# RWKV-7 and sliding-window decoder step: 16-row triangular inverses with a TensorE merge, and a third bonus buffer

## The chip, the cores and the metric

The kernel runs on one core of a Trainium2 chip. The metric is the device time of one execution in microseconds (us). The change is compared by the medians of runs made alike. The engines are TensorE (PE in the views; PEld is its weight load), VectorE (DVE), ScalarE (ACT), GpSimd (POOL) and SyncE (SP), which here issues almost all DMAs.

## The reference

One layer of a decoder for a prompt of 1024 tokens and eight samples of 8 tokens (1088 columns in all). A normalised input goes through one projection; half of its width feeds an RWKV-7 recurrence with 8 heads of 64, the other half attends within a window of 128. Both results are gated, projected, gated again and normalised. What matters here is the recurrence over tokens:

```python
    def step(S, inp):
        r_t, w_t, k_t, v_t, kk_t, a_t = inp
        sa = jnp.einsum('bhvk,bhk->bhv', S, kk_t)
        S = (S * w_t[:, :, None, :] - sa[..., None] * (kk_t * a_t)[:, :, None, :]
             + v_t[..., None] * k_t[:, :, None, :])
        return S, jnp.einsum('bhvk,bhk->bhv', S, r_t)
    ...
    S_fin, y = lax.scan(step, S0.astype(f32), xs)
    ...
    mixed = jnp.concatenate([o_r * jax.nn.silu(gate_r), o_a * jax.nn.silu(gate_a)], axis=-1)
    h = h + mixed @ w_out
    gate = jax.nn.sigmoid(rmsnorm(h, g_ple) @ w_pg)
    h = h + gate * (p @ w_pp)
```

## The kernel before, in words

**Stages.** The input is loaded, normalised and split into a high and a low part (`xh`, `xl`), so that each large product is three TensorE products (`gemm`, L157): high by high, low by high, high by low. `acc_k`, `acc_v`, `acc_q` and `acc_z` are projections; attention is interleaved with `acc_z`. Then come the recurrence (`chain`) and, around it, work that doesn't need its order: the gates (`acc_ga` and `acc_gr`, 12 groups of 24 products each) and the output part (`Late`: `acc_wa`, `acc_wr`, `acc_wg`, `pp`, and the final normalisation), whose weights pass through DRAM (`wo_dh`, `wo_dl`: half-megabyte stores, loaded back later). The products of the gates and of the output part, 128 x 128 by 384 or 320 columns, 1728 in all, are called gate products here.

**The chain.** The 1024 tokens are 16 chunks of 64. `steps` runs them one after the other: `ch` = state by `L` (L962); VectorE copies that to `rh` (L964); TensorE multiplies `rh` by the inverse in `B` (`ch<-rh`, L967); ScalarE and VectorE put the result into `sv`; TensorE multiplies `sv` by `K` (`cs`, L974), and VectorE adds that to the scaled state `sg`, which gives the next `sv`. "Step 9" is the ninth chunk, and its `ch<-rh` is the instruction by which the text dates it. `y`, the chunk's output, is normalised later (`finish`, from L918), where `bvl` is loaded and added as the bonus term.

**The inverse.** `prepare(u)` makes the operands of unit u: four chunks for u = 0 to 3, and the eight samples as one chunk for u = 4. Products `gram` give masked matrices `L` and `B`; per chunk and head there is a triangular 64 x 64 matrix to invert. In L836 to L896 this is done so: its diagonal 32 x 32 blocks (64 per unit, each twice with every other column of the inverse: 128 partitions) go through DRAM (`at_d`) into `a2` (called `a` in the views). VectorE eliminates row by row: 31 steps of a product into `tm` and a subtraction into `ti`, 62 instructions, recorded under the helper's line L55. ScalarE copies the result (`to`, L867), it goes through DRAM (`tt_d`, L869) back into `B` (L872), and the two blocks are merged: a transpose (L879), TE (L883), a copy `es` (L886), TF (L891) and a copy into `B` (L894). `a2`, `ti` and `tm` have one buffer each; `B`, `L` and `K` lie in two rings, unit u using ring u % 2, so unit 2 can only start when unit 0's steps have been read out of it.

**What sets the order.** `ORDER` = "P0 P1 V0 S0 P2 S1 P3 S2 G4 H0 P4 X4 S3" (L329) is the order in which the program is written: P is `prepare`, S `steps`, G the gates, H the late part, X the sample. The tile framework then schedules: it moves instructions within every engine's queue by its own timeline, with the chain's instructions at high priority. The program on each engine is therefore a fixed list, executed in order; an instruction that waits holds up all behind it on its engine. So where gate products stand between the chain's instructions was settled when the kernel was built.

## Time and profile before

| what | value |
|---|---|
| runs | 935.97, 939.41, 939.56 us |
| median | 939.41 us |
| profiled execution, its own time | 942.16 us |
| its span (first to last instruction) | 940.4 us |
| busy share PE / DVE / ACT / POOL | 88 / 67 / 40 / 39% |

The profile is one execution; its span is what all views divide. A busy share is a mean over stages with different limits, so the stages have to be read apart. In a table by stretch each line is one window: its length, the busy time of each engine with the number of its instructions in brackets, the granted clock of TensorE as a share of 2.4 GHz, the busy share of the DMA engines and GB/s. A timeline row is a start in us, a duration in us, the engine, the line of the kernel, the operation and its tiles; x16 are sixteen records in a row put into one. A product of 32-bit floats leaves two records. In the chain of waits each row is the start, the duration and what held the end.

### The profile page before, as it was taken

What the parts mean: (1) busy time and instruction counts of PE and PEld (TensorE: products, weight loads), DVE (VectorE), ACT (ScalarE), POOL (GpSimd) and SP (SyncE); (2) the same over time, 40 slices, a digit from 0 to 9 for tenths busy, and PEclk for the clock granted to TensorE, in tenths of its full rate; (3) what the DMA queues carried; (4) which work ended last, traced back from release to release, by engine and by line L of the source; (5) the groups of instructions that cost most, each with busy time, mean ns of one, the idle gap of its engine ahead of it and who ended that gap; (6) DMA issues with size and microseconds to landing.
All of it is one profiled execution on the core that took longest, in us unless ns stands there. A gap on an engine that the chain in (4) does not pass through costs nothing.

```text
span 940.4 us, 17475 instructions
## 1 busy us (share of the span) xinstructions
PE 828.5 (88%) x6352; PEld 738.4 (79%) x6352; DVE 632.7 (67%) x1511; ACT 372.5 (40%) x864; POOL 369.3 (39%) x494
## 2 busy tenths in 40 slices
PE   6978999999998989899799965987687989999994
PEld 5878999878886679788688854876577887899983
DVE  7856487777777453468774769588959766854464
ACT  6202086666666442652233332511333443322131
POOL 8548466665676422314231314315433353200000
PEclk9989999999999999899899975899797999999996
DMA  8013201322135447647644499686556879998882
GB/s 292 23 61 101 66 23 57 91 91 77 59 91 156 112 94 167 169 127 171 163 118 123 117 258 316 140 267 182 174 148 223 292 274 329 306 328 278 272 294 82
DMA packets 146007, 157.81 MB, mean 168 GB/s; under 512 B 59288, under 2 KB 115864, under 8 KB 145656
## 3 DMA queue, kind: packets, MB, share of 16 engines
q1 hardware_dynamic: 145104, 155.57, 54.6%
q10 hardware_dynamic: 816, 1.11, 0.4%
q8 instruction: 50, 0.82, 0.4%
q14 instruction: 37, 0.30, 0.1%
HBM read 106.77 MB, written 49.67 MB: 166 GB/s over the span
## 4 chain that ended last, share of the span: by engine, by line
PE 43%; DVE 25%; DMA 14%; ACT 6%; issue 6%; SPq 4%; POOL 2%; DVEq 0%; ACTq 0%; POOLq 0%
PE acc_z L157 6%; PE acc_gr L157 4%; PE acc_q L157 3%; DVE ti L55 3%; PE pp L1348 2%; DVE tm L55 2%; DMA a<-at_d 2%; ACT s L425 2%; PE ov L446 2%; PE acc_wg0g L157 1%; PE acc_wg3g L157 1%; DVE xl L58 1%; PE acc_wg7g L157 1%; PE acc_wg4g L157 1%; DVE s L421 1%
## 5 line engine op out<-in xcount | busy, mean ns | idle before, releaser
L157 PE MATMUL acc_z<-xh,wh_z 128*128 128x384 f32 (+1 forms) x312 | 65.1, 340 | 0.0
L157 PE MATMUL acc_z<-xl,wh_z 128*128 128x384 f32 (+1 forms) x312 | 62.6, 331 | 0.0
L157 PE MATMUL acc_z<-xh,wl_z 128*128 128x384 f32 (+1 forms) x312 | 62.5, 331 | 0.0
L157 PEld LDWEIGHTS acc_z<-xh,wh_z 128*128 128x128 f32 x312 | 53.7, 192 | 1.7 <-ACT pTS L505 0.2
L157 PEld LDWEIGHTS acc_z<-xh,wl_z 128*128 128x128 f32 x312 | 52.3, 188 | 1.0 <-issue 0.2
L157 PEld LDWEIGHTS acc_z<-xl,wh_z 128*128 128x128 f32 x312 | 52.6, 189 | 0.5
L55 DVE TENSOR_TENSOR ti<-ti,tm 128x56 f32<-128x56 f32 (+28 forms) x152 | 50.2, 330 | 3.5
L55 DVE TENSOR_TENSOR tm<-a,ti 128x56 f32<-128x56 f32 (+28 forms) x152 | 50.2, 330 | 3.5
L55 POOL TENSOR_TENSOR sg<-sv,GC 64x256 f32<-64x256 f32 x32 | 20.9, 652 | 63.0 <-DVE sv L55 61.1
L64 POOL TENSOR_SCALAR s<-s,sm 128x256 f32<-128x256 f32 (+1 forms) x64 | 34.6, 557 | 17.2 <-ACT pT L444 4.6
L1187 ACT ACTIVATE q<-hx 128x384 f32<-128x384 f32 (+1 forms) x41 | 20.8, 507 | 51.8 <-DVE hx L55 19.4
L800 PE MATMUL gram<-L,K 64*128 64x128 f32 x272 | 31.4, 324 | 4.9 <-issue 3.3
L55 POOL TENSOR_TENSOR wl_z<-wr_z,wh_z 128x1024 fp32r<-128x1024 f32 x13 | 31.3, 2406 | 10.1 <-ACT wh_z L146 4.8
L800 PEld LDWEIGHTS gram<-L,K 64*128 64x128 f32 x272 | 27.0, 219 | 9.5 <-issue 6.5
L55 DVE TENSOR_TENSOR zr<-acc_z,R 128x384 f32<-128x384 f32 (+2 forms) x52 | 21.7, 434 | 18.5 <-PE acc_z L157 18.2
L55 DVE TENSOR_TENSOR sq<-sq,q 128x384 f32<-128x384 f32 (+1 forms) x41 | 22.6, 552 | 15.1 <-ACT q L1187 14.7
L425 ACT ACTIVATE s<-s,sm 128x256 f32<-128x256 f32 (+1 forms) x64 | 30.9, 485 | 1.9 <-DVE sm L62 1.9
L446 PE MATMUL ov<-pT,vtok 128*64 128x512 f32 x60 | 31.2, 638 | 0.4 <-ACT pT L444 0.4
L1358 ACT ACTIVATE t<-t 128x384 f32<-128x384 f32 (+3 forms) x25 | 12.2, 494 | 46.8 <-DVE t L55 46.8
L55 POOL TENSOR_TENSOR gsa<-gsa,goa 128x384 f32<-128x384 f32 (+1 forms) x12 | 11.8, 985 | 45.8 <-DVE ti L55 27.0
L804 ACT COPY B<-L 64x512 f32<-64x512 f32 x34 | 20.9, 616 | 20.8 <-DVE L L55 19.9
L55 DVE TENSOR_TENSOR L<-gram,cst 128x512 f32<-128x512 f32 x34 | 22.5, 684 | 8.2 <-PE gram L800 8.0
(622 smaller groups left out, 2445.7 us busy)
## 6 DMA issues: line engine op xcount, KB each, us to landing
wr_z<-in_wz SPq DMA_DIRECT2D x13, 512.0 KB
L<-kq_d SPq DMA_DIRECT2D x24, 256.0 KB
sv<-vt_d SPq DMA_DIRECT2D x32, 128.0 KB
wh_wo<-wo_dh SPq DMA_DIRECT2D x8, 512.0 KB
wl_wo<-wo_dl SPq DMA_DIRECT2D x8, 512.0 KB
raw<-in_xT SPq DMA_DIRECT2D x8, 384.0 KB
kq_d<-KQ SPq DMA_DIRECT2D x8, 384.0 KB
bk_d<-BK SPq DMA_DIRECT2D x8, 384.0 KB
```

What stands on the lines that cost most here:

```text
L55: e.tensor_tensor(out, a, b, op=op)
L58: V.scalar_tensor_tensor(out, a, s, b, op0, op1)
L64: e.tensor_scalar(out, a, s1, s2, op0, op1)
L157: PE.matmul(acc[:, :n], w_[:, k0 + k, :], a_[c][:, k, :n], start=i + k == 0, stop=i == 2 and k == K - 1)
L421: V.tensor_tensor_reduce(s[:, j, :nk], sc[:, jj, :nk], mask, 1.0, -3e38, ADD, MAX, mx[:, j:j + 1])
L425: S.activation(s[:, j, :nk], s[:, j, :nk], AF.Exp, bias=m[:, 0, j:j + 1], accum_out=m[:, 2, j:j + 1])
L446: PE.matmul(ov[own, :], vtok[:, blk, own], pT[g].rearrange("p a b -> p (a b)"), start=pos == 0, stop=pos == nb - 1)
L800: PE.matmul(Gp[h][:, p], bk[hs, p], L[h][hs, p], start=True, stop=True)
L804: S.copy(r.B[hs, ci], L[h][hs])
L1187: e.S.square(q, h)
L1348: PE.matmul(pa, w[:, i], p[:, i], start=i + j == 0, stop=i == 1 and j == len(pr) - 1)
L1358: S.activation(t, t, AF.Tanh, scale=0.5)
```

## The change

The elimination works on 16 x 16 blocks: 128 of them fill the 128 partitions, with 16 columns each, and 15 steps take the place of 31. Two 16-row inverses then are merged into one of 32 rows in the way in which two of 32 are merged into one of 64: a product TC (L887 of the changed kernel), copies (`e1`), a product TD (L894), and copies with the factor -1 into `B`. TC and TD are 64 products of 16 x 16 each per unit, spread over four quadrants of TensorE's array. For them, transposed and plain 16 x 16 blocks are fetched from DRAM into `tq` by eight loads (L878, L879); `tt_d` gives way to `t1_d`, and the inverse goes back to `at_d` into its diagonal blocks. `fill` is no longer called in the elimination at steps 19 and 27, as there are none. The sample's 8-row matrices need no merge, and it returns before TC, TE and TF. Beside this, `bvl` has three buffers instead of two.

```diff
--- before.py
+++ after.py
@@ -744,13 +744,13 @@
     MUL, ADD, SUB, MAX = ALU.mult, ALU.add, ALU.subtract, ALU.max
     cst, par, ident, dp = e.cst, e.par, e.ident, e.dp
     kp = e.kp
-    early = ("a2", "ti", "tm", "rn", "q2")
+    early = ("a2", "ti", "tm", "rn", "q2", "tq")
     tl = lambda shape, tag, name, bufs: (kp if tag in early else e.kp3 if tag in ("sv", "sg", "rh") else e.kp2).tile(
         shape, F32, tag=tag, name=name, bufs=bufs)
     LO, HI = slice(0, 64), slice(64, 128)
 
     at_d = [dp.tile([64 if u < 4 else 16, 32, 32], F32, name=f"at_d{u}") for u in range(5)]
-    tt_d = [dp.tile([64 if u < 4 else 16, 32, 32], F32, name=f"tt_d{u}") for u in range(5)]
+    t1_d = [dp.tile([64 if u < 4 else 16, 16, 16], F32, name=f"t1_d{u}") for u in range(5)]
 
     units = [list(range(4 * u, 4 * u + 4)) for u in range(4)] + [[16]]
     src = lambda ch: (ch // 6, ch % 6)
@@ -827,49 +827,73 @@
         ncp = 4 * nch
         Bv = r.B.rearrange("p c a b -> p (c a) b")[:, :ncp]
         at4 = at_d[u].rearrange("(c r b) s t -> r b s c t", r=2, b=2)
-        tt4 = tt_d[u].rearrange("(c r b) s t -> r b s c t", r=2, b=2)
+        t14 = t1_d[u].rearrange("(c r b) t s -> r b t c s", r=2, b=2)
+        diag = lambda d, q: d[..., 16 * q:16 * q + 16, 16 * q:16 * q + 16]
         rows = lambda pr, b: slice(64 * pr + 32 * b, 64 * pr + 32 * b + 32)
-        a2 = tl([128, 32, 32], "a2", f"a2_{u}", 1)
-        rn = tl([128, 32], "rn", f"rn{u}", 1)
-        HO = max(H, 32)
-        P2 = slice(0, 2 * HO)
-        for x in range(0, 2 * HO, H):
-            DMAQ("rn").dma_start(rn[x:x + H], e.ss_d[chs[0]:chs[0] + nch].rearrange("c p r (b t) -> (c p r b) t", b=2))
+        row16 = lambda pr, b: slice(64 * pr + 32 * b, 64 * pr + 32 * b + 16)
+        quad = [(pr, b) for pr in range(2) for b in range(2)]
+        a2 = tl([128, 16, 16], "a2", f"a2_{u}", 1)
+        rn = tl([128, 16], "rn", f"rn{u}", 1)
+        P2 = slice(0, 2 * H)
+        HQ = [slice(H * q, H * q + H) for q in range(2)]
+        for q in range(2):
+            DMAQ("rn").dma_start(rn[HQ[q]], e.ss_d[chs[0]:chs[0] + nch].rearrange(
+                "c p r (b q t) -> q (c p r b) t", b=2, q=2)[q])
         ts(V, rn[P2], rn[P2], 1e-24, None, MAX)
         V.reciprocal(rn[P2], rn[P2])
-        for pr in range(2):
-            for b in range(2):
-                DMAQ("at").dma_start(at4[pr, b], Bv[rows(pr, b), :, 32 * b:32 * b + 32])
-        for x in range(0, 2 * HO, H):
-            DMAQ("at").dma_start(a2[x:x + H], at_d[u])
-        ti = tl([128, 32, 16], "ti", f"ti{u}", 1)
+        for pr, b in quad:
+            DMAQ("at").dma_start(at4[pr, b], Bv[rows(pr, b), :, 32 * b:32 * b + 32])
+        for q in range(2):
+            DMAQ("at").dma_start(a2[HQ[q]], diag(at_d[u], q))
+        ti = tl([128, 16, 16], "ti", f"ti{u}", 1)
         G.memset(ti[P2], 0.0)
 
-        tif = ti.rearrange("p t c -> p (t c)")
-        for h in range(2):
-            hh = slice(HO * h, HO * h + HO)
-            G.tensor_copy(tif[hh, 16 * h:16 * h + 496:33], rn[hh, h::2])
-        tt(V, a2[P2], a2[P2], rn[P2].unsqueeze(1).to_broadcast([2 * HO, 32, 32]), MUL)
-        tm = tl([128, 136], "tm", f"tm{u}", 1)
-        for j in range(31):
-            e_ = (j | 7) + 1 if smp else 32
-            c0 = (j // 8) * 4 if smp else 0
-            nr, ncol = e_ - j - 1, j // 2 + 1 - c0
+        G.tensor_copy(ti.rearrange("p t c -> p (t c)")[P2, 0::17], rn[P2])
+        tt(V, a2[P2], a2[P2], rn[P2].unsqueeze(1).to_broadcast([2 * H, 16, 16]), MUL)
+        tm = tl([128, 64], "tm", f"tm{u}", 1)
+        for j in range(15):
+            e_ = (j | 7) + 1 if smp else 16
+            c0 = (j // 8) * 8 if smp else 0
+            nr, ncol = e_ - j - 1, j + 1 - c0
             if nr == 0:
                 continue
             w = tm[P2, 0:nr * ncol].rearrange("p (a b) -> p a b", a=nr)
-            tt(V, w, a2[P2, j, j + 1:e_].unsqueeze(2).to_broadcast([2 * HO, nr, ncol]),
-               ti[P2, j, c0:c0 + ncol].unsqueeze(1).to_broadcast([2 * HO, nr, ncol]), MUL)
+            tt(V, w, a2[P2, j, j + 1:e_].unsqueeze(2).to_broadcast([2 * H, nr, ncol]),
+               ti[P2, j, c0:c0 + ncol].unsqueeze(1).to_broadcast([2 * H, nr, ncol]), MUL)
             tt(V, ti[P2, j + 1:e_, c0:c0 + ncol], ti[P2, j + 1:e_, c0:c0 + ncol], w, SUB)
             if fill and j % 8 == 3:
                 e.fill(("t", u))
-        to = tl([128, 16, 32], "q2", f"to{u}", 2)
+        to = tl([128, 16, 16], "q2", f"to{u}", 2)
         S.copy(to[P2].rearrange("p c t -> p t c"), ti[P2])
-        for h in range(2):
-            DMAQ("tt").dma_start(tt_d[u].rearrange("i (c h) t -> h i c t", h=2)[h], to[HO * h:HO * h + H])
-        for pr in range(2):
-            for b in range(2):
-                DMAQ("tt").dma_start(Bv[rows(pr, b), :, 32 * b:32 * b + 32], tt4[pr, b])
+        for q in range(2):
+            DMAQ("tt").dma_start(diag(at_d[u], q), to[HQ[q]])
+        for pr, b in quad:
+            DMAQ("tt").dma_start(Bv[rows(pr, b), :, 32 * b:32 * b + 32], at4[pr, b])
+        if smp:
+            return r
+
+        DMAQ("tt").dma_start(t1_d[u], ti[HQ[0]])
+        tq = tl([128, 2, 16, 16], "tq", f"tq{u}", 1)
+        for pr, b in quad:
+            DMAQ("tt").dma_start(tq[row16(pr, b), 0], t14[pr, b])
+            DMAQ("tt").dma_start(tq[row16(pr, b), 1], at4[pr, b, 16:32, :, 16:32])
+        e1 = tl([128, 16, 16], "q2", f"e1_{u}", 2)
+        bank = lambda nm: ps("ov", nm, 1)[:, 0:256].rearrange("p (a b) -> p a b", a=16)
+        up = lambda b: slice(32 * b + 16, 32 * b + 32)
+        p1 = bank(f"TC{u}")
+        for i in range(ncp):
+            for pr, b in quad:
+                a = row16(pr, b)
+                PE.matmul(p1[a, i], Bv[a, i, up(b)], tq[a, 0, i], start=True, stop=True)
+        for pr, b in quad:
+            S.copy(e1[row16(pr, b)], p1[row16(pr, b)])
+        p2 = bank(f"TD{u}")
+        for i in range(ncp):
+            for pr, b in quad:
+                a = row16(pr, b)
+                PE.matmul(p2[a, i], e1[a, i], tq[a, 1, i], start=True, stop=True)
+        for pr, b in quad:
+            S.activation(Bv[row16(pr, b), :, up(b)], p2[row16(pr, b)], AF.Copy, scale=-1.0)
 
         t1 = tl([128, 16, 32], "q2", f"t1_{u}", 2)
         es = tl([128, 16, 32], "q2", f"es_{u}", 2)
@@ -933,7 +957,7 @@
             y = ys[ci]
             tt(G, y, y, w[:, ci].unsqueeze(2).to_broadcast([128, 4, 64]), MUL)
             tt(G, y, y, lnw, MUL)
-            bv = tl([128, 4, 64], "bv", f"bvl{ch}", 2)
+            bv = tl([128, 4, 64], "bv", f"bvl{ch}", 3)
             DMAQ("bvl").dma_start(bv, e.vt_d[ch % 2, ch // 2].rearrange("h t p v -> (h t) p v"))
             tt(V, bv, bv, bq[:, ci].unsqueeze(2).to_broadcast([128, 4, 64]), MUL)
             tt(V, y, y, bv, ADD)
```

**VectorE, end of unit 0's elimination.** `L_3683<-gram_7` and `L_3684<-gram_7` are the masked matrices of the fourth chunk of unit 1. Before:

```order
L55 TENSOR_TENSOR L_3683<-gram_7_4033,cst 128x512
L55 TENSOR_TENSOR tm_3811<-a_0_3794,ti_3806 128x126
L55 TENSOR_TENSOR L_3684<-gram_7_4034,cst 128x512
L55 TENSOR_TENSOR ti_3806<-ti_3806,tm_3811 128x21x6
L55 TENSOR_TENSOR gsa_6183<-acc_ga_2_6158,R 128x320
L55 TENSOR_TENSOR tm_3811<-a_0_3794,ti_3806 128x120
L55 TENSOR_TENSOR ti_3806<-ti_3806,tm_3811 128x20x6
```

There nineteen more pairs follow. After the change the same place reads:

```order
L55 TENSOR_TENSOR tm_3810<-a_0_3794,ti_3806 128x28
L55 TENSOR_TENSOR ti_3806<-ti_3806,tm_3810 128x2x14
L55 TENSOR_TENSOR L_3683<-gram_7_4149,cst 128x512
L55 TENSOR_TENSOR tm_3810<-a_0_3794,ti_3806 128x15
L55 TENSOR_TENSOR L_3684<-gram_7_4150,cst 128x512
L55 TENSOR_TENSOR ti_3806<-ti_3806,tm_3810 128x15
L55 TENSOR_TENSOR gsa_6647<-acc_ga_2_6622,R 128x320
```

The pair on 15 elements beside `L` is the last one of unit 0.

**TensorE behind step 8, after the change.** `TC_5216` and `TD_5285` are unit 2's, `cs_5639` is step 8, and the `ch<-rh` of step 9 stands some thirty rows further on:

```order
L1014 MATMUL cs_5639<-sv_5586,B_3686 64x64 x8
L157 MATMUL acc_gr_0_7113<-xh_78,wh_gr_7078 128x384 x4
L157 MATMUL acc_gr_0_7113<-xl_81,wh_gr_7078 128x384 x8
L157 MATMUL acc_gr_0_7113<-xh_78,wl_gr_7079 128x384 x5
L887 MATMUL TC_5216<-tq_5206,B_3690 16x16 x61
L157 MATMUL acc_gr_0_7113<-xh_78,wl_gr_7079 128x384 x3
L157 MATMUL acc_gr_1_7144<-xh_79,wh_gr_7072 128x384 x8
L157 MATMUL acc_gr_1_7144<-xl_82,wh_gr_7072 128x384 x8
L157 MATMUL acc_gr_1_7144<-xh_79,wl_gr_7073 128x384 x3
L800 MATMUL gram_14_5798<-L_3683,K_3685 128x128
L800 MATMUL gram_14_5799<-L_3684,K_3685 128x128
L894 MATMUL TD_5285<-tq_5206,e_2_5215 16x16 x64
```

So gates of `acc_gr` stand between TC and TD of unit 2, where `acc_wa` of the late part stood before.

**SP, the loads of `tq` for unit 3, after the change.** `wh_woa` and `wl_woa` are late weights on their way to DRAM:

```order
L869 DMA at_d_3676<-to_5895 64x16x16
L1046 DMA L_3688<-kq_d 64x512 x2
L1328 DMA wo_dh<-wh_woa_7853 128x2x512
L1328 DMA wo_dl<-wl_woa_7854 128x2x512
L1328 DMA wo_dh<-wh_woa_7861 128x2x512
L878 DMA tq_5904<-t_d_3681 16x16x16 x3
L871 DMA B_3686<-at_d_3676 32x16x32 x4
L879 DMA tq_5904<-at_d_3676 16x16x16 x3
L878 DMA tq_5904<-t_d_3681 16x16x16
L879 DMA tq_5904<-at_d_3676 16x16x16
```

Three half-megabyte stores are issued between the store of the inverse and the loads that follow it (`t_d` is the program's `t1_d`).

## Rows read from the trace of the kernel before

**Rows 1.** The page, busy time, share of the span and instructions.

```profile
PE 828.5 (88%) x6352; PEld 738.4 (79%) x6352; DVE 632.7 (67%) x1511; ACT 372.5 (40%) x864; POOL 369.3 (39%) x494
```

**Rows 2.** Table by stretch: length, PE, PEld, DVE, ACT, POOL, PEclk, DMA share, GB/s.

```profile
0.00:470.00 470.00, 429.89 (x2669) 380.24 (x2670) 315.73 (x712) 223.72 (x557) 242.99 (x343) 0.97 0.39 110
470.00:554.00 84.00, 79.48 (x1002) 68.56 (x1001) 51.90 (x129) 28.23 (x61) 21.33 (x34) 0.96 0.52 137
554.00:611.00 57.00, 40.08 (x405) 34.90 (x402) 43.22 (x107) 24.45 (x52) 20.43 (x26) 0.73 0.83 239
611.00:731.00 120.00, 93.07 (x1153) 81.87 (x1151) 97.74 (x280) 33.98 (x66) 43.78 (x52) 0.87 0.64 195
731.00:940.00 209.00, 185.99 (x1134) 172.81 (x1132) 124.11 (x286) 62.11 (x128) 40.76 (x40) 0.96 0.81 276
```

**Rows 3.** Timeline of TensorE, the products of steps 8 and 9.

```profile
554.44 0.68 PE L967 MATMUL ch<-rh,B 64*64 64x64 f32 x16
...
611.53 0.68 PE L967 MATMUL ch<-rh,B 64*64 64x64 f32 x16
```

**Rows 4.** Timeline of VectorE, `rh` of steps 6 and 7.

```profile
530.70 0.42 DVE L964 COPY rh<-ch 128x256 f32<-128x256 f32 x1 [2.14 <-PE ch L962]
...
541.13 0.42 DVE L964 COPY rh<-ch 128x256 f32<-128x256 f32 x1 [0.97 <-PE ch L962]
```

**Rows 5.** Table by stretch for tile `ti`: DVE, ACT, POOL, PEclk, DMA, GB/s.

```profile
0.00:940.00 940.00, 100.35 (x304) 5.57 (x5) 5.06 (x15) 0.94 0.55 168
554.00:611.00 57.00, 23.26 (x54) 1.10 (x1) 0.94 (x3) 0.73 0.83 239
611.00:731.00 120.00, 32.46 (x118) 2.28 (x2) 0.94 (x3) 0.87 0.64 195
```

**Rows 6.** Timeline of VectorE, unit 2's elimination.

```profile
566.29 2.68 DVE L55 TENSOR_TENSOR tm<-a,ti 128x133 f32<-128x133 f32 x1
...
574.43 0.29 DVE L55 TENSOR_TENSOR ti<-ti,tm 128x136 f32<-128x136 f32 x1
...
588.01 0.17 DVE L55 TENSOR_TENSOR ti<-ti,tm 128x16 f32<-128x16 f32 x1
```

**Rows 7.** Timeline of VectorE, unit 0's elimination and the transpose behind it.

```profile
408.60 0.18 DVE L55 TENSOR_TENSOR tm<-a,ti 128x31 f32<-128x31 f32 x1
...
412.57 0.25 DVE L55 TENSOR_TENSOR tm<-a,ti 128x81 f32<-128x81 f32 x1
...
420.83 0.68 DVE L55 TENSOR_TENSOR L<-gram,cst 128x512 f32<-128x512 f32 x1
...
440.93 0.17 DVE L55 TENSOR_TENSOR ti<-ti,tm 128x16 f32<-128x16 f32 x1
...
449.45 0.69 DVE L879 STREAM_TRANSPOSE t<-B 32x512 f32<-32x512 f32 x1
```

**Rows 8.** Timeline of TensorE, TE of unit 0.

```profile
451.53 1.19 PE L883 MATMUL TE<-t,B 32*32 32x32 f32 x62
```

**Rows 9.** Timeline of SP, unit 0's inverse going out and back.

```profile
440.92 1.12 SPq L844 DMA_DIRECT2D a<-at_d  x2
442.26 1.26 SPq L869 DMA_DIRECT2D tt_d<-to  x2
...
446.86 1.94 SPq L872 DMA_DIRECT2D B<-tt_d  x4
```

**Rows 10.** Tile `TE`: the copies; ns least/median/most, first and last start us, forms.

```profile
L886 ACT COPY es<-TE x10: 257/578/579, 452.8 to 695.8; 32x512 f32<-32x512 f32 x8, 32x128 f32<-32x128 f32 x2
```

**Rows 11.** Chain of waits over the span: start, duration, what held it.

```profile
397.53 3.03 DMA at_d<-B
401.21 4.49 DMA a<-at_d
...
564.83 9.06 DMA wo_dh<-wh_woa
...
843.32 4.16 PE acc_wg3g L157 x24
```

## The prediction

> **What bounds the kernel now.** I read the page first. TensorE is busy 88% of the span, VectorE 67%, so TensorE looks like the bound [rows 1]. The table by stretch says where this fails [rows 2]. I cut the span at the chain's products `ch<-rh` of steps 1, 8, 9 and 16 (two of them are shown), because they are serial: sixteen chunks, each needing the state of the chunk before [rows 3]. Five stages follow. To step 1 (470 us) TensorE is busy 430 of 470 us. Steps 1 to 8 take 84 us and are nearly full. Step 8 to step 9 takes 57 us, with TensorE busy for 40 at a granted clock of 0.73 and VectorE for 43. Steps 9 to 16 take 120 us; VectorE is busy for 98 of them, TensorE for 93. After step 16 TensorE is busy 186 of 209 us.
>
> How fast could the chain go? Where it waits for no inverse, `rh` follows `rh` after 541.13 - 530.70 = 10.4 us [rows 4]. So 57 us at step 9 is a stall. What ends last there is the inverse of unit 2: the `ch<-rh` of step 9 needs `B`, `B` needs TF, TF needs the last `ti`. Of VectorE's 43 us, 23.3 are `ti` and `tm` instructions; in the next stage they are 32.5 of 98 [rows 5]. They cost more than their size says: at 566.29 one `tm` of 133 columns takes 2.68 us, while later one of 136 takes 0.29 [rows 6].
>
> **The change, part by part.** *The recurrence.* A unit has 62 `ti`/`tm` instructions now, and 30 after the change; the sample has 56 (31 steps less three with no row below in their block) and 28 afterwards. Altogether 304 instructions take 100.4 us, a mean of 330 ns [rows 5]. The new ones are 15 to 64 elements wide (7 to 16 in the sample); widths of 31 and 81 take 0.18 and 0.25 us undisturbed [rows 7], so 0.22 in the middle, and 0.22 x 1.32 = 0.29 if disturbed as much as the present ones (0.330 against the 0.25 of width 81, a middling one for them). With 148 instructions that is 33 to 43 us: VectorE loses 57 to 67 us. The multiply of `a` falls from 1024 to 256 columns, about 1 us a unit, and is not counted. None of it shortens the span by itself: it does where the inverse is what ends last.
>
> *The merge.* Per unit there are 64 products TC and 64 TD of 16 x 16, not in the trace. The nearest row is TE: 62 records (31 products) in 1.19 us, 19 ns a record, 0.038 us a product [rows 8]. From below: half of that, if four quadrants overlap as well as TE's two do. From above: 0.085 us, the pitch of the 64-column products `ch<-rh` (16 records, 8 products, in 0.68 us) [rows 3]. I take 0.038, the nearest in shape: 128 x 0.038 = 4.9 us a unit, 19.5 for four (10 to 43.5). The Trainium skill ("TensorEngine Tiling (Array Packing)", Instruction Overhead) gives each matmul some 60 cycles however few its columns. By that rule, as an estimate at 2.4 GHz, a record costs 25 ns and the four units 1024 x 25 ns = 25.6 us, and the sum below would be 6 us higher; the row's 19 ns lies under the rule, so I keep the row.
>
> *The path from the last `ti` to the chain.* In unit 0 it runs: the last `ti` ends at 441.1 and the transpose begins at 449.45 [rows 7], 8.4 us later; between them two stores are issued from 442.26 and four loads of `B` from 446.86 [rows 9]. The merge adds one store and eight `tq` loads on SP (nine issues; four take 1.94 us, so 4.4), TC 2.4, four copies of 256 columns (a copy of 128 columns takes 257 ns, of 512 takes 578 [rows 10]: 0.36 each, 1.5 together), TD 2.4, four more copies 1.5: +12.2 us. So TC can run some 12.5 us after the last `ti`, and the transpose comes 20.6 us after it.
>
> Now the stages; a gate product costs 4.16 us for 24, 0.173 each [rows 11]; their number ahead of a step is counted in the two orders.
>
> 1. *To step 1.* TensorE's order has 354 gate products ahead of it now and 240 then: 114 x 0.173 = -19.7, with +4.9 for TC and TD: -15. Does the inverse allow it? Unit 0's `ti` runs from 408.6 to 441.1 now [rows 7]; then its last pair stands right behind the `L` of 420.83, so it ends near 422, plus 20.6, plus 6 to 7 for transpose, TE, copy, TF and copy: 449. TensorE is last; I take **-14** (bounds -17 and 0, the latter if SP is late with `sv`).
> 2. *Steps 1 to 8.* 222 gate products become 189 (-5.7), TC and TD of unit 1 come in (+4.9). But `a` has one buffer, so unit 1 loads after unit 0's recurrence, as the issue at 440.92 shows [rows 9]; its `ti` ends near 455, its TC is ready near 468, and TensorE's order puts two TC between `ch<-rh` and `cs` of step 1 (456): the chain waits there some 10 us. Seven steps of 10.4 and this wait are 83. I take 86, **+2** (-5 to +12).
> 3. *Step 8 to 9.* Unit 2's `ti` ends shortly after step 8 now, no longer 34 us behind it (588.0 against 554.4) [rows 3, 6]. Its TC, ready some 15 us after step 8, blocks TensorE; behind the last TC stand 108 gate products (18.8), gram, `ytr`, TD, TE and TF (some 10): 15 + 2.4 + 29 = 46. I take 47, **-10** (37 for TensorE's work alone, to 60).
> 4. *Steps 9 to 16.* 236 gate products become 172 (-11.1), TC and TD add 4.9; VectorE loses about 17 of its 32.5 us. Seven steps are 73; unit 3's TC stands inside step 12, and its `tq` loads are issued behind three half-megabyte stores; I give the stall and the sample's products ahead of TF 29 us, so 102, **-18** (-28 to 0).
> 5. *After step 16.* The work left out above stands here: 844 gate products become 1002, 158 x 0.173 = 27.3, on an engine that is 89% busy: **+28** (from +14, if half of it fills the 23 idle us, to +31 at this stage's busy share).
>
> Sum: 940.4 - 14 + 2 - 10 - 18 + 28 = 928. The profiled execution took 942.16 us itself, 2.75 above the median of the runs, 939.41; 12 us off that gives **927**. SP's 36 further issues in four units lie in stages 1 to 4 and are counted in the path. The third `bvl` buffer removes a wait of the load for `y` of the chunk two before; all of it lies beside the chain, which does not read `bvl`: nothing, and at the worst SP is blocked a few us less.
>
> **The rivals.**
> - *More is gained* (0.20). The moved gate products fill stage 5's waits: half of 28 saved, and TC and TD cost half: 927 - 14 - 9 = 904. For it: TensorE idles 23 us there [rows 2]. Against it: those waits end on weights and VectorE, not on missing work.
> - *No change* (0.13). The merge's path is as long as the recurrence was: stage 3 gains nothing, 937. For it: +12.2 us of path on each unit. Against: 23 us of `ti`/`tm` go to about a half of that.
> - *Slower: TensorE blocked by TC* (0.15). TensorE takes its instructions in order, so a late `tq` stops gates and chain alike. The place is TC of units 2 and 3, where half-megabyte stores share the queue; one wait for such a store was 9.06 us [rows 11]. Twice that is +18: 945. It decides from about 6 us of extra delay in each. The Trainium skill ("DMA: Bandwidth & Descriptors", Specifications) asks for runs of 512 B for full rate, and `tq`'s are 64 B. The trace does not show such a penalty: `at_d<-B` with 128 B runs took 3.03 us, `a<-at_d` with 4 KB runs 4.49 [rows 11].
> - *Slower: TC and TD are dear* (0.07). At 0.085 us a product they cost 43.5 us, not 19.5: 951.
>
> **How the numbers follow.** The forecast has 0.45, and its own range is 915 to 940. A measurement tells 0.5%, 4.7 us, from no change. Faster: 0.40 of the forecast and 0.20, 0.60. Same: 0.05 of it and 0.13, 0.18. Slower: 0.22. The range 904 to 950 takes in the rivals' times but the last, and leaves out about a fifth: that one, and stages that all fall to one bound.
>
> **What would show it.** VectorE's busy time near 570 us; `ch<-rh` of step 1 near 456, of step 8 near 542, of step 9 near 589, of step 16 near 691; then 237 us with TensorE some 90% busy. Right on the mechanism: the stretch from step 8 to 9 no longer ends on `ti`. Wrong if TensorE waits for `tq` by 10 us or more in each unit, if TC and TD take much over 5 us a unit, or if the time after step 16 stays near 209.

## The result, and the profile after

The changed kernel takes 965.09 us (median of 4; 960.39 to 966.96) against 939.48: a ratio of 1.0255, interval 1.0227 to 1.0282. It is slower by 2.5%. The forecast was 927, its range 904 to 950. The profiled execution took 960.39 us, span 958.2, at the lower end of the runs; the one of the kernel before was at the upper end. So the medians differ by 25.6 us, the two profiles by 17.8, and no view shows the other 8.

Part 1 of the page after the change [rows 1]:

```profile
PE 847.9 (88%) x7344; PEld 755.6 (79%) x7344; DVE 583.7 (61%) x1353; ACT 382.4 (40%) x892; POOL 369.5 (39%) x489
```

The table by stretch, cut as before at the `ch<-rh` of steps 1, 8, 9 and 16 [rows 2]:

```profile
0.00:462.20 462.20, 415.77 (x2812) 365.82 (x2812) 289.30 (x659) 224.33 (x560) 236.07 (x337) 0.95 0.38 104
462.20:550.90 88.70, 80.59 (x1231) 70.47 (x1231) 49.56 (x118) 32.90 (x74) 25.02 (x35) 0.89 0.53 139
550.90:596.50 45.60, 41.08 (x652) 36.91 (x652) 23.36 (x61) 19.18 (x45) 9.82 (x15) 0.89 0.51 124
596.50:705.90 109.40, 90.65 (x1355) 77.06 (x1354) 64.14 (x183) 27.53 (x57) 41.47 (x55) 0.80 0.67 195
705.90:958.20 252.30, 219.81 (x1297) 205.32 (x1296) 157.38 (x334) 78.51 (x157) 57.10 (x48) 0.94 0.81 274
```

The chain gets shorter, but by less than forecast: step 16 begins at 705.9, 25 us earlier and not 40. Step 8 to 9 takes 45.6 instead of 57, as forecast. All of the 25 us, and 18 more, goes into the stretch behind step 16: 252.3 us against 209. TensorE's busy time rises by 19.4 us, and its idle time stays what it was (940.4 - 828.5 = 111.9 before, 958.2 - 847.9 = 110.3 after): in the profiles, the longer span is longer busy time.

Where the last stretch loses time stands in its head; two windows of 14 us, same columns:

```profile
720.00:734.00 14.00, 11.67 (x56) 10.77 (x56) 12.37 (x27) 6.21 (x11) 9.79 (x11) 0.88 1.03 372
734.00:748.00 14.00, 7.74 (x42) 7.15 (x42) 14.00 (x23) 7.38 (x15) 6.45 (x6) 0.98 0.93 326
```

TensorE idles for 8.6 of these 28 us while VectorE is busy for 26.4. The chain of waits goes there through VectorE's `sq`, `or` and `ul`, the head of the output part. What comes ahead of it is later too. The answers for tiles `acc_gr`, `acc_wa` and `acc_wg0g` (count: least/median/most ns, first and last start in us), first of the kernel before:

```profile
L157 PE MATMUL acc_gr<-xh,wl_gr x96: 302/334/688, 452.9 to 539.1; 128*128 128x384 f32 x64, 128*128 128x320 f32 x32
L157 PE MATMUL acc_wa<-mah,wh_woa x32: 333/337/687, 569.3 to 646.5; 128*128 128x384 f32 x32
L157 PE MATMUL acc_wg0g<-uh,wh_wg0g x24: 307/338/667, 723.5 to 883.8; 128*128 128x384 f32 x16, 128*128 128x320 f32 x8
```

and of the changed one:

```profile
L157 PE MATMUL acc_gr<-xh,wl_gr x96: 304/334/687, 503.4 to 601.5; 128*128 128x384 f32 x64, 128*128 128x320 f32 x32
L157 PE MATMUL acc_wa<-mah,wh_woa x32: 333/337/443, 621.6 to 711.2; 128*128 128x384 f32 x32
L157 PE MATMUL acc_wg0g<-uh,wh_wg0g x24: 307/336/667, 749.4 to 902.5; 128*128 128x384 f32 x16, 128*128 128x320 f32 x8
```

The gates end 62 us later, the output part's first products start 52 us later and its first `acc_wg0g` 26 us later. From there to the end it is 940.4 - 723.5 = 216.9 us before and 208.8 after. In all twenty profiles of this study that distance is 207 to 230 us, which is a spread as wide as the loss to be explained.

What the merge itself takes on TensorE, by groups (busy us, mean ns of one | idle before, what ended it):

```profile
L887 PE MATMUL TC<-tq,B 16*16 16x16 f32 x512 | 8.3, 185 | 9.4 <-DMA B<-at_d 5.3 <-DMA tq<-t_d 2.6 <-issue 1.3
L894 PE MATMUL TD<-tq,e 16*16 16x16 f32 x512 | 5.5, 181 | 3.7 <-issue 3.3 <-ACT e L889 0.4
```

13.8 us busy and 13.1 us of waiting just ahead.

### The profile page after: what moved, and what is told of

Its sections match the earlier page's. It is cut to its first block, busy times and chain, and to the rows that moved or that the text cites. A ratio compares the mean times of both kernels' runs of the same rounds, so it can differ in the third digit from the quotient of the medians.

```text
span 958.2 us, 19378 instructions
## 1 busy us (share of the span) xinstructions
PE 847.9 (88%) x7344; PEld 755.6 (79%) x7344; DVE 583.7 (61%) x1353; ACT 382.4 (40%) x892; POOL 369.5 (39%) x489
## 4 chain that ended last, share of the span: by engine, by line
PE 26%; DMA 8%; DVE 8%; SPq 3%; issue 2%; ACT 2%; POOL 1%; DVEq 0%; ACTq 0%; POOLq 0%
PE pp L1372 2%; PE acc_gr L157 2%; PE acc_wa L157 2%; PE acc_wg5g L157 2%; PE acc_wg0g L157 1%; PE acc_wg3g L157 1%; PE acc_wg1g L157 1%; PE acc_wg7g L157 1%; DMA bvl<-vt_d 1%; DVE y L55 1%; PE acc_wg6g L157 1%; PE acc_wr0c L157 1%; DVE ti L55 1%; SPq L845 1%; PE acc_wr1c L157 1%
## 5 line engine op out<-in xcount | busy, mean ns | idle before, releaser
L55 POOL TENSOR_TENSOR sg<-sv,GC 64x256 f32<-64x256 f32 x32 | 20.6, 642 | 76.7 <-DVE sv L55 75.3
L55 DVE TENSOR_TENSOR sq<-sq,q 128x384 f32<-128x384 f32 (+1 forms) x41 | 28.6, 697 | 12.5 <-ACT q L1211 12.2
L1382 ACT ACTIVATE t<-t 128x384 f32<-128x384 f32 (+3 forms) x25 | 12.2, 494 | 54.3 <-DVE t L55 54.3
L446 PE MATMUL ov<-pT,vtok 128*64 128x512 f32 x60 | 31.2, 637 | 0.4 <-ACT pT L444 0.4
L800 PE MATMUL gram<-L,K 64*128 64x128 f32 x272 | 26.2, 311 | 5.0 <-DVE L L55 3.3
L800 PEld LDWEIGHTS gram<-L,K 64*128 64x128 f32 x272 | 21.7, 207 | 8.6 <-DVE L L55 3.5
L986 PE MATMUL ch<-sv,L 128*64 128x64 f32 x256 | 16.8, 253 | 12.2 <-DVE sv L55 6.2
L986 PEld LDWEIGHTS ch<-sv,L 128*64 128x64 f32 x256 | 12.8, 158 | 17.4 <-DVE sv L55 7.2
L55 DVE TENSOR_TENSOR a<-a,rn 128x256 f32<-128x256 f32 (+1 forms) x5 | 2.1, 422 | 39.6 <-DMA a<-at_d 39.6
L55 POOL TENSOR_TENSOR gsa<-gsa,goa 128x384 f32<-128x384 f32 (+1 forms) x12 | 11.5, 957 | 37.7 <-DMA goa<-oa_d 13.2
```

What stands on the lines that cost most here:

```text
L55: e.tensor_tensor(out, a, b, op=op)
L446: PE.matmul(ov[own, :], vtok[:, blk, own], pT[g].rearrange("p a b -> p (a b)"), start=pos == 0, stop=pos == nb - 1)
L800: PE.matmul(Gp[h][:, p], bk[hs, p], L[h][hs, p], start=True, stop=True)
L986: PE.matmul(X1[hs, p], L[h][:, p, 0:64], sv[:, h, p], start=True, stop=True)
L1382: S.activation(t, t, AF.Tanh, scale=0.5)
```

## The experiments

Three theories were tested first. **Displacement**: the time is lost because 158 gate products stand behind the chain. **Price**: it is what TC and TD and their waits cost. **Bonus**: the third buffer does it. The scheduler makes a new order for every edit, so each expectation gives the gate products ahead of steps 1, 8, 9 and 16. Ratios are against the kernel before in the same session (its median was 939.5 to 941.8 us in them). The last three columns are the start of step 16's `ch<-rh`, the gate products that stand behind it, and the time from it to the end of the span.

| run | us | ratio, interval | last `acc_gr` | first `acc_wg0g` | step 16 | products behind | us behind |
|---|---|---|---|---|---|---|---|
| kernel before | 939.5 | | 539.1 | 723.5 | 731.4 | 844 | 209.0 |
| changed kernel | 965.1 | 1.026, 1.023-1.028 | 601.5 | 749.4 | 705.9 | 1002 | 252.3 |
| e1 two bonus buffers | 965.2 | 1.024, 1.018-1.030 | 606.0 | 754.0 | 710.3 | 1002 | 257.5 |
| e2 third buffer alone | 947.3 | 1.0054, 1.003-1.008 | 537.7 | 716.5 | 728.7 | 837 | 213.3 |
| e3 `tq` on ScalarE's queue | 951.0 | 1.008, 1.005-1.011 | 550.7 | 731.7 | 741.1 | 840 | 209.1 |
| e4 units 2, 3, sample | 943.7 | 1.003, 1.000-1.006 | 540.0 | 730.8 | 729.1 | 864 | 214.7 |
| e5 output part early | 964.8 | 1.024, 1.020-1.028 | 600.6 | 747.7 | 743.1 | 864 | 221.4 |
| e6 way back on ScalarE's queue | 953.1 | 1.012, 1.010-1.015 | 531.3 | 730.2 | 740.4 | 840 | 209.0 |
| e7 wide products | 942.9 | 1.002, 1.000-1.005 | 571.6 | 724.2 | 718.5 | 864 | 222.9 |
| e8 = e4, way back as e6 | 955.1 | 1.014, 1.011-1.017 | 534.6 | 735.7 | 745.0 | 840 | 209.2 |
| e9 gates written early | 950.2 | 1.009, 1.006-1.012 | 547.6 | 723.9 | 744.0 | 821 | 206.4 |
| e10 before, gates early | 939.0 | 0.998, 0.996-1.001 | 526.4 | 710.4 | 729.5 | 819 | 202.7 |
| e11 no merge | 923.1 | 0.982, 0.979-0.985 | 537.4 | 717.5 | 690.1 | 944 | 234.0 |
| e12 gates first | 969.3 | 1.031, 1.028-1.034 | 526.5 | 742.7 | 755.5 | 831 | 208.8 |
| e13 products twice (e9) | 982.0 | 1.044, 1.038-1.051 | 560.9 | 761.2 | 774.2 | 831 | 206.1 |
| e14 products without loads | 939.4 | 0.998, 0.995-1.001 | 534.1 | 724.9 | 720.8 | 864 | 219.5 |
| e15 no merge, gates early | 937.5 | 0.997, 0.994-0.999 | 531.7 | 709.4 | 724.6 | 825 | 214.5 |
| e16 sample alone | 931.9 | 0.989, 0.986-0.992 | 542.7 | 714.3 | 729.7 | 826 | 201.6 |
| e17 wide products (e9) | 948.9 | 1.008, 1.005-1.011 | 546.7 | 723.3 | 738.0 | 825 | 210.8 |
| e18 = e16, gates early | 929.2 | 0.990, 0.982-0.998 | 529.4 | 708.6 | 725.5 | 816 | 201.3 |

The last two columns go together: in all twenty profiles the stretch behind step 16 lasts 0.244 to 0.260 us for each gate product left behind it, whatever the recurrence did ahead of it.

**e1 and e2: the bonus buffer.**

```diff
-            bv = tl([128, 4, 64], "bv", f"bvl{ch}", 3)
+            bv = tl([128, 4, 64], "bv", f"bvl{ch}", 2)
```

> The changed kernel with two bonus buffers again. Displacement theory (the time is lost because 158 gate products, and with them the head of the output part, stand behind the chain): TensorE's order has 240, 429, 553 and 726 gate products ahead of steps 1, 8, 9 and 16, as good as the changed kernel's, so 958 to 968 us, and the stretch after step 16 again near 252 us against 209 before. Price theory (the 128 products TC and TD per unit and the waits for tq cost what was lost, wherever the gates stand): the same 958 to 968. Bonus theory (the third buffer lets loads of bvl go ahead and hold VectorE or SP): under 950.

For e2 the kernel before gets the 3:

> The kernel before with the third bonus buffer alone. Its order has 354, 576, 705 and 891 gate products ahead of steps 1, 8, 9 and 16 (354, 576, 648 and 884 in the kernel before). Displacement theory: nothing is displaced, 935 to 943 us, and the stretch after step 16 stays within 5 us of 209. Price theory: the same, 935 to 943. Bonus theory: 950 or more.

Taking the buffer away changes nothing (965.2). Alone it costs 0.5%, some 5 us (947.3, between the ranges of the theories), by one comparison whose order differs too. The bonus theory falls.

**e3: the loads of `tq` on another queue.**

```diff
-DQ = {"lp": "A"}
+DQ = {"lp": "A", "tq": "A"}
...
-            DMAQ("tt").dma_start(tq[row16(pr, b), 0], t14[pr, b])
+            DMAQ("tq").dma_start(tq[row16(pr, b), 0], t14[pr, b])
```

> The changed kernel, but the eight loads of tq per unit are issued on ScalarE's queue instead of SP's. All merge work is kept (512 products TC and TD). What the order makes of it: 342, 576, 684 and 888 gate products ahead of steps 1, 8, 9 and 16, that is as in the kernel before and not as in the changed one. Displacement theory: the stretch after step 16 falls from 252 back to within 8 us of 209, and the time to 930 to 950, though TensorE's busy time stays near 848. Price theory by TensorE's work: it stays at 955 to 968, as the work is the same. Price theory by waits for tq on SP: 940 to 950 with TensorE's idle time ahead of TC (20 us in the changed kernel) mostly gone.

951.0, and the stretch after step 16 is back at 209:

```profile
741.10:950.20 209.10, 187.05 (x1129) 172.68 (x1128) 128.93 (x288) 63.39 (x130) 41.28 (x40) 0.96 0.82 275
```

All merge work is there (TensorE busy 847.1 us), so 14 of the 25.6 us aren't the price of TensorE's work. A part may still be the price of the waits: ahead of TC and TD TensorE idles for 7.5 us here and for 13.1 in the changed kernel. (The 20 us in the expectation count its weight loads as well.) 10 remain; the time is just above the displacement theory's range.

**e4: units 2 and 3 alone** (`tq` lies in the unused part of `a2`).

```diff
+        if u in (2, 3, 4):
+            ...
+        else:
+            ...
```

> The 16-row elimination and merge in units 2 and 3 (and the 16-row blocks in the sample) alone; units 0 and 1 as before; three bonus buffers. 353, 576, 624 and 864 gate products ahead of steps 1, 8, 9 and 16. Displacement theory: 928 to 942 us, as the stretch from step 8 to 9 is shortened to 40 to 50 us and only 20 products more than before stand behind step 16. Price theory: half of what was lost, 945 to 955.

943.7, but not for the reason expected: step 8 to 9 takes 64.9 us. Unit 2's elimination ends at 569.8 and its transpose begins at 603.2, by the timeline of VectorE:

```profile
569.58 0.17 DVE L55 TENSOR_TENSOR ti<-ti,tm 128x15 f32<-128x15 f32 x1
603.22 1.42 DVE L955 STREAM_TRANSPOSE t<-B 32x512 f32<-32x512 f32 x2
```

Between them SP issues half-megabyte stores of late weights among the inverse's own stores and loads, at a DMA share of 1.04 from 566 to 590:

```profile
571.74 1.31 SPq L1380 DMA_DIRECT2D wo_dh<-wh_woa  x2
573.47 2.23 SPq L872 DMA_DIRECT2D at_d<-to  x2
575.78 2.90 SPq L1380 DMA_DIRECT2D wo_dl<-wl_woa  x1
...
585.33 2.58 SPq L874 DMA_DIRECT2D B<-at_d  x4
```

The elimination was shortened, and the chain now waits for the way back through DRAM (TC starts at 590.2, some 20 us after the elimination) and for the merge (13 us more to the transpose).

**e5: the displaced products put ahead of step 16.**

```diff
-ORDER = "P0 P1 V0 S0 P2 S1 P3 S2 G4 H0 P4 X4 S3"
+ORDER = "P0 P1 V0 S0 P2 S1 P3 G4 S2 H0 F9 P4 X4 S3"
```

> The changed kernel with all its work; only the order in which the program is written differs: the gates are written ahead of unit 2's steps and nine pieces of the output part's head ahead of the sample and of unit 3's steps. 240, 431, 552 and 864 gate products stand ahead of steps 1, 8, 9 and 16: as in the changed kernel up to step 9, and 138 more ahead of step 16. Displacement theory: the stretch after step 16 falls from 252 to 212 to 224 us, the steps 9 to 16 get longer by less than that, and the time is 938 to 955. Price theory (the merge's products and waits, which are all still there): 958 to 968, as whatever leaves the last stretch comes back ahead of it.

The displacement theory falls as it was put. With 138 products fewer in it the last stretch is shortened by 31 us to 221, as it said, but steps 9 to 16 get longer by 40, and the time stays, in the price theory's range:

```profile
593.70:743.10 149.40, 120.37 (x1495) 103.82 (x1494) 84.45 (x213) 41.60 (x82) 54.36 (x61) 0.84 0.70 210
743.10:964.50 221.40, 194.44 (x1158) 180.12 (x1158) 137.79 (x305) 65.40 (x133) 45.28 (x42) 0.94 0.79 267
```

In the table, the runs near 965 (e1, e5) have their last `acc_gr` past 600, and their first `acc_wg0g` near 750. Hence a further theory, the **train theory**: the gates' end sets when the output part can begin, and the end follows 207 to 230 us after its first `acc_wg0g`.

**e6, e8: the inverse's way back on ScalarE's queue.**

```diff
-DQ = {"lp": "A"}
+DQ = {"lp": "A", "tt": "A"}
```

> The changed kernel with all its work; all DMAs of the inverse's way back (the stores at_d and t1_d, the loads of B and tq) are issued on ScalarE's queue instead of SP's. 398, 588, 729 and 888 gate products ahead of steps 1, 8, 9 and 16. Displacement theory: the stretch after step 16 stays within 8 us of 209, and the time is 938 to 953. If the way back through SP's queue is what a unit still waits for: the stretch from step 8 to 9 is under 60 us (70.8 with tq alone on ScalarE's queue), and the time under 945. Price theory by TensorE's work: 955 or more.

> The 16-row elimination and merge in units 2 and 3 and in the sample alone, three bonus buffers, and the inverse's way back on ScalarE's queue in all units. 396, 576, 672 and 888 gate products ahead of steps 1, 8, 9 and 16. With the same on SP's queue the inverse of unit 2 was eliminated at 569.8 us, but its TC began at 590.2 and its transpose at 603.2, behind half-megabyte stores on the queue. If that queue is the new wait: the transpose comes within 20 us of the last elimination, the stretch from step 8 to 9 falls from 64.9 to under 55, and the time from 943.7 to 930 to 940. If the transfers themselves are slow beside the stores (the DMA engines are full there): no more than 5 us of it, 939 to 947.

Another queue is no cure: step 8 to 9 takes 66.5 us in e6 and 76.2 in e8, which is 11 us slower than e4. In e8 the last `ti` of unit 2 starts at 568.6 and its TC only at 608.1, so SP's queue alone isn't the wait; which part of the way back is, these runs don't separate.

**e9, e10, e12: the gates' place.**

```diff
-ORDER = "P0 P1 V0 S0 P2 S1 P3 S2 G4 H0 P4 X4 S3"
+ORDER = "P0 P1 V0 S0 G4 P2 S1 P3 S2 H0 P4 X4 S3"
```

> The changed kernel with all its work; the gates are written ahead of unit 2's preparation and not behind unit 2's steps. 288, 576, 708 and 907 gate products ahead of steps 1, 8, 9 and 16; the last of acc_gr stands behind step 6, as in the kernel before, and not behind step 9. Train theory (the output part can only begin when the gates are done, and the end comes about 217 us after the first acc_wg0g in all kernels so far, 209 to 226): acc_gr ends near 545 instead of 601, the first acc_wg0g is at 720 to 735, and the time 935 to 952. Price theory (the merge's products and its waits on TensorE): 955 to 968, as none of that is taken away.

> The kernel before, its gates written in the same place as in the run above: 356, 576, 681 and 909 gate products ahead of steps 1, 8, 9 and 16 (354, 576, 648 and 884 without). The control for it. Train theory: acc_gr ends within 10 us of the 539 of the kernel before, so 932 to 945. If the place of the gates were a gain of its own, whatever the inverse: under 930.

In e12, G4 stands ahead of S0:

> The changed kernel with all its work; the gates are written ahead of unit 0's steps. 288, 691, 768 and 897 gate products ahead of steps 1, 8, 9 and 16; acc_gr ends behind step 2. Train theory, taken to its end: acc_gr ends near 510, but the output part also needs the chunks of the recurrence, so the first acc_wg0g is no earlier than 715 and the time is 932 to 950. Price theory: 955 to 968.

e9 falls where the train theory put it (`acc_gr` ends at 547.6, the first `acc_wg0g` is at 723.9) and outside the price theory's range: with every instruction of the merge, 950.2. It doesn't single out the gates' end, as the edit gives a new order throughout, with 181 products fewer behind step 16. In the kernel before the same edit does nothing to the time (0.998), though its gates end 13 us earlier (526.4, not within 10 as expected) and its first `acc_wg0g` comes 13 us earlier too: that far the train theory fails. e12 shows the limit. Gates that end at 526 don't help when they stand in the chain's way: steps 1 to 8 take 144 us, the first `acc_wg0g` comes at 742.7, the time is 969.3, and both theories missed it. From the last `acc_gr` to the first `acc_wg0g` it is 148 us in the changed kernel, 184 before and 216 in e12, so the gates' end alone sets no date.

**e7, e11, e13, e14, e15, e17: what the merge costs.** e11 cuts the merge out, e15 does so at e9's order:

```diff
-        DMAQ("tt").dma_start(t1_d[u], ti[HQ[0]])
...
-            S.activation(Bv[row16(pr, b), :, up(b)], p2[row16(pr, b)], AF.Copy, scale=-1.0)
+            S.activation(Bv[row16(pr, b), :, quad_up(b)], Bv[row16(pr, b), :, quad_up(b)], AF.Copy, scale=0.0)
```

> The changed kernel with the merge of 16-row blocks left out of the computation: no t1_d, no tq, no TC and TD; the off-diagonal 16-row blocks are set to zero in its place by four of the eight copies, so that the inverse is one of the diagonal blocks only. 349, 576, 588 and 784 gate products ahead of steps 1, 8, 9 and 16; acc_gr ends behind step 6. It shows what the shorter elimination would bring if the merge were free. Price theory: 915 to 930, 30 to 50 us under the changed kernel. Train theory: the gates end as early as in the kernel before, so 930 to 942, and no better than the kernel before by more than 10, as what follows the gates is the same work.

> No merge (left out as before: off-diagonal 16-row blocks zero), with the gates written early as in the run whose control it is: 321, 576, 681 and 903 gate products ahead of steps 1, 8, 9 and 16. If the merge's price doesn't hang on the order: 920 to 930, which is 20 to 30 us under 950. If it was the order that made the difference between 950 and 923: 935 or more.

e13 does each product twice:

```diff
-                PE.matmul(p1[a, i], Bv[a, i, up(b)], tq[a, 0, i], start=True, stop=True)
+                for _ in range(2):
+                    PE.matmul(p1[a, i], Bv[a, i, up(b)], tq[a, 0, i], start=True, stop=True)
```

> The run with the gates written early, with each product TC and TD done twice into the same place (1024 in place of 512). 308, 576, 717 and 897 gate products ahead of steps 1, 8, 9 and 16 (288, 576, 708 and 907 without). Product theory (TC and TD are worth what they are busy, 13.8 us, and more): 962 to 972. Wait theory (TensorE is held up by what TC and TD wait for, and the products lie in the shadow of the waits): 948 to 960.

e14 keeps the products and takes the loads away:

```diff
-                PE.matmul(p2[a, i], e1[a, i], tq[a, 1, i], start=True, stop=True)
+                PE.matmul(p2[a, i], e1[a, i], cst[a, 0:16], start=True, stop=True)
```

> The changed kernel with the 512 products and the eight copies per unit, but without the store t1_d and the loads of tq: TC and TD read a constant tile, and the last copies write zero, so the off-diagonal 16-row blocks of the inverse are left out of the computation. TensorE has nothing to wait for at TC. 380, 576, 644 and 864 gate products ahead of steps 1, 8, 9 and 16. Wait theory: 923 to 936, nearly as without the merge. Product theory: 937 or more, the 923 without the merge and the 13.8 us or more of the products.

e7 and, at e9's order, e17 have wide products:

```diff
-                PE.matmul(p1[a, i], Bv[a, i, up(b)], tq[a, 0, i], start=True, stop=True)
+            PE.matmul(p1[a], Bv[a, 0, up(b)], tq[a, 0], start=True, stop=True)
```

> The changed kernel with TC and TD of a unit in 4 products of 256 columns each in place of 64 of 16 columns; left out of the computation: the merge then takes one block of the quadrant for all sixteen, so the inverse's off-diagonal 16-row blocks are not those of the reference. Loads and copies stay. 279, 543, 578 and 864 gate products ahead of steps 1, 8, 9 and 16. Displacement theory: the stretch after step 16 is 212 to 224 us, the time 938 to 952. Price theory: TensorE's busy time falls by 10 to 14 us from 848 and the time by the same, to 950 to 955; if the products themselves are all of the loss, 945 or less with the stretch after step 16 still over 240.

> The run with the gates written early (950 us), with TC and TD of a unit in 4 products of 256 columns each in place of 64 of 16; left out of the computation: one block of a quadrant is taken for all sixteen, so the off-diagonal 16-row blocks are not the reference's. All loads, copies and waits stay. 264, 576, 684 and 903 gate products ahead of steps 1, 8, 9 and 16 (288, 576, 708 and 907 without). If the number of products is what costs: 935 to 943, near the 937 without a merge. If loads, copies and waits are: 946 to 952.

e11 (923.1) lies in the price theory's range and below the train theory's 930 to 942; e15 (937.5) says that this depends on the order. At one order the merge costs 950.2 - 937.5 = 12.7 us (e9, e15; two sessions, in which the kernel before differs by 1.4). Doubling its 512 products costs 31.8 more, more than either theory had, and the groups of e13 say how: busy time rises by 12.6 us and the waiting ahead by 23.8, most of it "issue". First e9:

```profile
L887 PE MATMUL TC<-tq,B 16*16 16x16 f32 x512 | 7.9, 180 | 4.7 <-DMA tq<-t_d 2.3 <-DMA B<-at_d 1.9 <-PE cs L998 0.3
L894 PE MATMUL TD<-tq,e 16*16 16x16 f32 x512 | 5.4, 177 | 0.3 <-issue 0.3
```

and e13:

```profile
L888 PE MATMUL TC<-tq,B 16*16 16x16 f32 x1024 | 14.1, 181 | 20.1 <-issue 11.9 <-DMA B<-at_d 6.4 <-DMA tq<-t_d 1.5
L896 PE MATMUL TD<-tq,e 16*16 16x16 f32 x1024 | 11.8, 183 | 8.7 <-issue 8.7
```

e17 (948.9, in its range for loads, copies and waits) and e14 (939.4, above the wait theory's range) don't separate the parts: wide products are busy no less (TC 12.2 us in e17), and e14's order is neither e11's nor e15's. Two orders without a merge, whose gates end within 6 us of each other, differ by 14 us (923.1 and 937.5). Part 1 of their pages, e11 and then e15, says where it lies:

```profile
PE 824.6 (89%) x6320; PEld 735.6 (80%) x6320; DVE 594.2 (64%) x1353; ACT 377.7 (41%) x876; POOL 367.4 (40%) x489
PE 838.6 (89%) x6320; PEld 748.5 (80%) x6320; DVE 590.8 (63%) x1353; ACT 377.4 (40%) x876; POOL 367.6 (39%) x489
```

The same 6320 records keep TensorE busy 14.0 us longer in e15, while it idles for 99.5 and 100.5 us. The mean granted clock is 0.942 in e11 and 0.929 in e15; that the clock is the whole of it isn't shown. So an order alone can be worth as much as the gain of e9. The merge's price is known at one order only, and the bare elimination is worth 3 us at one and 17 at the other. e7 (942.9, with 222.9 us behind step 16) fits the displacement theory's number, and with its last `acc_gr` at 571.6 lies between the two groups of the table.

**e16, e18: the part that needs no merge.** The kernel before with the 16-row path in unit 4 alone; e18 with e9's `ORDER` too.

```diff
+        if u in (4,):
+            ...
+        else:
+            ...
```

> The kernel before with the 16-row path in the sample's unit alone, which needs no merge (28 instead of 56 ti and tm, no TE and TF there), two bonus buffers. 354, 576, 648 and 902 gate products ahead of steps 1, 8, 9 and 16. Every theory: the sample lies off the chain, so 933 to 942; a gain beyond 0.5% (under 935) would mean that VectorE's time beside steps 9 to 16 counts by itself.

> The kernel before with the 16-row path in the sample's unit alone (932 us) and the gates written early (939 by itself, no difference). 356, 576, 681 and 912 gate products ahead of steps 1, 8, 9 and 16. If both are as they were alone: 928 to 935. If the gain of the sample's part hung on the order it came with: 936 to 943.

931.9 and 929.2 us: both beat the kernel before and the changed one. The first `acc_wg0g` comes 9 and 15 us earlier than before. The two ratios can't be told apart. The reason given in e16's expectation, VectorE's time, isn't borne out by part 1 of its page:

```profile
PE 824.0 (88%) x6320; PEld 734.0 (79%) x6320; DVE 637.1 (68%) x1481; ACT 370.9 (40%) x860; POOL 370.0 (40%) x493
```

VectorE has 30 instructions fewer and is busy no less (637.1 us, 632.7 before). The order has 18 gate products fewer behind step 16, and the stretch there is 7.4 us shorter.

## Why the prediction was wrong

*Right:* the recurrence. `ti` and `tm` take 38.6 us in 148 instructions (forecast 33 to 43), 61.7 less. The way back: unit 0's last `ti` starts at 421.1 and its transpose at 443.3, 22.2 us (forecast 20.6). Step 8 to 9 is 11.5 us shorter (forecast 10), and TC of unit 2 runs from 12 us after step 8 (forecast 15). TC and TD are busy for 13.8 us, under the 19.5 taken. By the rule of the Trainium skill ("TensorEngine Tiling (Array Packing)", Instruction Overhead), some 60 cycles for each matmul, it would have been 25.6, an estimate; the trace disagrees on the busy time, at 13.5 ns a record. The margin of e13 (31.8 us for 1024 records, 31 ns each) is over both, but most of that is waiting. One reading was off: the 0.29 us for 136 columns [rows 6] are a `ti` and not a `tm`; the sum doesn't use it.

*Wrong.* The five stretches summed to 928 us, and the profile's span is 958.2. Of these 30 us step 5 is 15, steps 1, 2 and 4 together are 16, and step 3 gives 1.5 back.

*First:* step 5, "the work left out above stands here". It measured +43.3, not +28, beyond its bound of 31. The term that was mis-sized is the price of a product left behind: 0.173 us, what one keeps TensorE busy. The stretch behind step 16 goes by 0.244 to 0.260 us a product in all twenty profiles, and did so before the change (209.0 us for 844, 0.248). At that pitch the 158 products are 39 us. They fill no idle time, as the lower bound supposed: TensorE's idle time there rises by 9 us, in the head, where VectorE is full, and its busy time by 34 instead of 27.

So the 25 us by which step 16 came earlier were work left out, and cost more at the end than they had saved. Put back, the work takes the lead away: e5 has 138 products fewer behind step 16, which comes 37 us later. With the merge and about as many products behind as in the kernel before (840, 840 and 821 in e3, e6 and e9, 844 before), step 16 comes at 740 to 744 us and not at 731. A sum of stretches in which products move freely could not show this. The rival "more is gained" made the same mistake.

*Second:* step 1 gave -8.1 for -14. TensorE's busy time fell by 14.4 us (430.2 to 415.8), as summed; what the sum had at nothing is that TensorE idles 6.3 us longer. The timeline of TensorE names waits around unit 0's merge, and, ahead of step 1, not the inverse but the load of `sv`, which a bound of the step had named. (The last row names GpSimd's `wl_gr`, which `ch` doesn't read; the last load of `sv` was issued at 457.83, behind stores of unit 1's inverse.)

```profile
430.13 0.23 PE L887 MATMUL TC<-tq,B 16*16 16x16 f32 x2 [2.35 <-DMA B<-at_d]
...
438.67 1.22 PE L894 MATMUL TD<-tq,e 16*16 16x16 f32 x122 [0.44 <-ACT e L889]
441.28 0.22 PE L894 MATMUL TD<-tq,e 16*16 16x16 f32 x6 [1.40 <-issue]
...
444.12 0.28 PE L907 MATMUL TE<-t,B 32*32 32x32 f32 x2 [2.13 <-DVE ti L55]
...
457.40 0.44 PE L986 MATMUL ch<-sv,L 128*64 128x64 f32 x2 [2.80 <-DMA sv<-vt_d]
460.54 1.09 PE L986 MATMUL ch<-sv,L 128*64 128x64 f32 x14 [2.69 <-POOL wl_gr L55]
```

Step 4 gave -10.5 for -18: unit 3's merge is not the reason, as the step it stands in takes 31.2 us (632.8 to 664.0; forecast 10.4 + 29), but the other six take 13.0 on average. The 10.4 of a step, read from one pair of steps of the kernel before, was too small here.

Step 2, +4.6 for +2, is right by luck: the wait of 10 us at TC ahead of `cs` of step 1 did not come (TensorE waits 1.3 us there, and step 1 to 2 takes 8.3), while the six steps behind it take 13.4 each. A part of that is the clock:

```profile
438.00:444.00 6.00, 2.14 (x133) 1.54 (x131) 2.41 (x10) 3.10 (x9) 0.00 (x0) 0.96 0.61 100
444.00:450.00 6.00, 5.88 (x78) 5.42 (x79) 4.33 (x19) 2.68 (x6) 0.61 (x2) 0.50 0.55 141
...
456.00:462.00 6.00, 1.53 (x16) 1.22 (x16) 0.33 (x1) 2.12 (x3) 2.90 (x4) 0.60 0.62 108
462.00:468.00 6.00, 4.46 (x122) 3.76 (x124) 1.80 (x5) 0.38 (x1) 1.22 (x2) 0.50 0.53 102
468.00:474.00 6.00, 4.67 (x172) 4.17 (x168) 2.74 (x5) 2.82 (x7) 1.86 (x2) 0.50 0.52 173
474.00:480.00 6.00, 5.47 (x90) 5.20 (x91) 3.38 (x8) 1.50 (x4) 2.41 (x4) 0.50 0.44 118
```

Behind the merge's wait at 438 to 444 and the wait ahead of step 1, TensorE works at 0.50, its lower level of 1.2 GHz. The 20.5 us busy at 0.50 in these windows would be about 10 at the full clock, an estimate: 3 of it ahead of step 1 and 7 behind.

*The rivals.* "Slower: TensorE blocked by TC" (0.15) had the sign and a part of the cause: TensorE does wait at TC and TD, for 13.1 us in all. But its place was wrong. Half-megabyte stores stand ahead of unit 3's `tq` loads alone, and TensorE waits for DMAs 1.7 us at that TC, less than at unit 0's (2.35) and unit 2's (2.5). No rival had a product cost more at the end than ahead of it.

So of the 25.6 us, about 15 come back in another order (e9, with e3 and e6 agreeing at 951 and 953) and about 10 stay: the merge, less what the shorter elimination brings (950.2 with, 937.5 without, 939 to 942 before). That it is the gates' place which makes these orders better is argued, not shown: e11 and e12 lie outside that theory's ranges, in e10 gates that end 13 us earlier gain nothing, and e11 and e15 differ by as much with gates that end alike. That the scheduler put the gates late because the chain was ready earlier in its plan is argued too, not tested.

## What to carry to other kernels

Before you shorten a stalled chain, ask what fills its stalls. Work that an earlier chain leaves behind has to be paid at the end, so price it by the last stretch's length over its products in the trace before (here 0.248 us), not by what one product keeps its engine busy (0.173). An edit also reorders a scheduled program, so run it in two or three orders before you credit it or blame it. The part that brings no new work, here the sample's, gained 1% in both orders that were tried; why, these runs don't settle.

## What the runs showed that was not expected

Long runs of 16 x 16 products pause where the view names nothing to wait for. The timeline of TensorE in e13:

```profile
430.57 1.55 PE L888 MATMUL TC<-tq,B 16*16 16x16 f32 x137
434.41 1.16 PE L888 MATMUL TC<-tq,B 16*16 16x16 f32 x107 [2.29 <-issue]
...
441.31 2.69 PE L896 MATMUL TD<-tq,e 16*16 16x16 f32 x253
446.79 0.24 PE L896 MATMUL TD<-tq,e 16*16 16x16 f32 x3 [2.79 <-issue]
```

After 137 and 253 records come pauses of 2.3 and 2.8 us; in the changed kernel 1.4 us after 122 (unit 0's TD) and 1.9 after 53 (unit 2's), and none within the 128 of unit 3's. The cause wasn't tried and stays open.
